# Large tiles on multiples of 256 bytes, the second pair's q and v in pools of their own, and another memory layout for the second MLP stage

## The chip, the cores and the metric

The kernel runs on one core of a Trainium2 chip. The metric is the device time of one execution in microseconds (us). Five engines matter here, with the names that the profile gives them: PE (TensorE, matrix products; PEld is its loading of the stationary operand), DVE (VectorE), ACT (ScalarE), POOL (GpSimd) and SP (SyncE, which issues most of the DMAs, in the order of its program). SBUF, the memory on the chip that the engines read and write, has 128 partitions; "address" below means a byte address within a partition.

## The reference

One encoder layer over a sequence of 1024 positions with a model width of 1024, in float32:

```
h    = RMSNorm(x)
[z | xBC | dt | q | k | v] = h @ W_in                     # 1024 x 5664
ssd  : depthwise conv of 5 taps and SiLU on xBC, Mamba-2 scan in both directions
       (8 chunks of 128, 16 heads of 64, 2 groups), + D*x, * SiLU(z), grouped RMSNorm
na   : 16 heads of 64, RMSNorm on q and k, attention of every position to an 8 x 16 window
       of the 16 x 64 grid, with a learned bias
x    = x + concat(ssd, na) @ W_out                        # 2048 x 1024
x    = x + relu(RMSNorm(x) @ W1)^2 @ W2                   # 1024 x 4096 and 4096 x 1024
```

## The kernel before

Every large product is made from float32 operands split into a high and a low part of type float32r: three matmuls (high x high, high x low, low x high) go into the same PSUM tile. In a matmul one operand is stationary (128 x 128, loaded by PEld) and one is moving (128 rows, 512 columns in the large products, which are 2048 bytes of a partition). A split costs an ACT copy (`wh`, `hTh`, the first half of `ahl`; line 367) and a subtraction on DVE or POOL (`wl`, second half of `ahl`; line 368).

Stages, in the order of time:

1. Input projection and scan (to about 620 us). The normalised input lies transposed in `hTh` and `hTl`; weights come in `wraw` tiles. The scan of the state-space part runs between the projections. `rcol` holds the norm's factor of each position and is read until the last piece of the projection is split (lines 919 and 920). `q`, `k` and `v` go to DRAM.
2. Attention for the 8 pairs of heads and three quarters of the output projection (to about 905 us). `pair_loads` fetches `q`, `k`, `kl` and `v` of a pair into one of two sets of tiles: set 0 in pool `b0`, set 1 in pool `b1`. The output projection's matmuls (`po`) take `wh`, `wl` from pool `wp` as moving and `yh`, `yl` from pool `yp` as stationary operand.
3. Last quarter of the output projection, norm, and first MLP product (to 1266 us): 8 blocks of 7 products (a Winograd form of Strassen's scheme; order 1, 2, 6, 5, 7, 3, 4) of 24 matmuls each. Moving operand `h` in the tiles `h1` to `h7` (pools `hA` and `b0`), stationary `wh`, `wl` from `wp`. The seven results of each pair of blocks are stored in `act_dr`.
4. Second MLP product (to the end): 4 blocks of 7 products of 48 matmuls. For each product two stationary pairs `ahl` come from activations (`ar`, loaded from `act_dr`), and two moving pairs `wh`, `wl` from the weights (`wraw`, for products 6, 5, 7, 4 combined by subtractions on DVE, lines 1911 to 1916). The tiles are taken from rings in turn: `ahl` from `a1`, `a1`, `a2`, `a2`, `a3`, `a3`; the weights' halves from `wy` three times and `wp` three times.

Stages 1 to the beginning of 3 are written as tasks with costs, due times and an earliest time (`since`, in us relative to the time at which PE is planned to end the stage before); a planner in the program orders them, and this order is kept on each engine. The rest of 3 and all of 4 is ordered by the framework, which simulates the engines and puts an instruction where its operands and its memory are free.

SBUF is given out from two sides. Pools of the left side stack upwards from address 4224: `cp`, `wp`, then what a stage needs (`hp`, `sp`; `x2p`; `hq`; `x1`, `a3`). Pools of the right side stack downwards from 229344: `b0` first, then `yp` and others, in stage 3 `wq` and `hA`, in stage 4 `rb`, `wy`, `x0`, `ra`, `a2`, `a1`, `ar`. A tile in a new pool waits for the users of whatever lay in its memory before. `cp` is 928 bytes long with `rcol` in it, so `wp` begins at 5152, which is 32 beyond a multiple of 256; all further large tiles of the left side that the matmuls of 512 columns read begin 32 beyond such a multiple as well. Those of the right side that the matmuls of 512 columns read begin 224 beyond one, because 229344 does, and because the sizes in between are multiples of 256.

The tiles of stage 4 lie where these of stage 3 were: `rb` on `h6` and `h5`, `wy` on the raw weights `wq`, `x0` on `h4`, `ra` on `h3`, `a2` and `a1` on `h2` and `h1`, `ar` on `h7`, `x1` and `a3` on `hq`. The first two `wraw` of stage 4 are those of `wp`.

Of the kernel before, what the change touches and what calls it, by code (L numbers as in the profile page):

```python
# [10 lines left out]
F32 = mybir.dt.float32  # L11
F32R = mybir.dt.float32r
# [7 lines left out]
P = 128  # L20
T = 1024
D = 1024
NT = T // P
# [207 lines left out]
def hymba_block(  # L231
# [27 lines left out]

    cp = ctx.enter_context(tc.tile_pool(name="cp", bufs=1))  # L260
    wp = ctx.enter_context(tc.tile_pool(name="wp", bufs=1))
    ps = ctx.enter_context(tc.tile_pool(name="ps", bufs=1, space=PSUM))
    dr = ctx.enter_context(tc.tile_pool(name="dr", bufs=1, space=DRAM))

# [130 lines left out]
        emit = lambda: nc.sync.dma_start(out(), src())  # L395
        plan.task("SP", 0.45, emit, reads=reads, writes=writes, size=size, **more)

    def tiles_of_pair(i, pool):
        make = {
            f"{t}{i}": partial(pool.tile, [P, 2, T], F32R, tag=t, name=t, bufs=1)  # L400
            for t in ("q", "k", "kl")
        }
        make[f"v{i}"] = partial(pool.tile, [P, NT, 2, P], F32R, tag="v", name="v", bufs=1)
        return make

    kls = {}
# [1 line left out]
    def pair_loads(plan, p, after=()):  # L408
        Buf, part, task = plan.buf, plan.part, plan.task
        i = p % 2  # L410
        free = dict(since=4.0) if p == 1 else {}
        q, k, v = Buf(f"q{i}"), Buf(f"k{i}"), Buf(f"v{i}")
        qp = {(j, a): part(q) for j in range(2) for a in range(2)}
        kp = [part(k) for _ in range(2)]
        for j in range(2):
            for a in range(2):
                load_task(
                plan,
                    256,
                    partial(lambda j, a: q.t[a * HD : (a + 1) * HD, j].bitcast(F32), j, a),  # L420
                    partial(lambda j, a: q_dr[p // 4, a ^ j, p % 4, j * HD : (j + 1) * HD], j, a),
                    reads=after, writes=[qp[j, a]],
                    name="q",
                    **free,
                )
            load_task(
                plan,
                512,
                partial(lambda j: k.t[j * HD : (j + 1) * HD].bitcast(F32), j),
                partial(lambda j: k_dr[p // 4, 0, p % 4].rearrange("(h d) t -> d h t", h=2), j),  # L430
                reads=after, writes=[kp[j]],
                name="k",
                **free,
            )
        if p < 2:
            kls[p] = Buf(f"kl{i}"), []
            for j in range(2):
                half_, whole = part(kls[p][0]), kls[p][0]
                kls[p][1].append(half_)
                task("POOL", 1.0, partial(lambda j, b: nc.gpsimd.memset(b.t[HD * (1 - j) : HD * (2 - j), j].bitcast(F32), 0.0), j, whole), writes=[half_], name="kl0", **free)  # L440
        kl, klp = kls[i]
        for j in range(2):
            hp = slice(HD * j, HD * j + HD)
            load_task(plan, 256, partial(lambda hp, j: kl.t[hp, j].bitcast(F32), hp, j), partial(lambda hp: k_dr[p // 4, 1, p % 4, hp], hp), reads=after, writes=[klp[j]], name="kl", **free)
        load_task(
                plan,
            1024,
            lambda: v.t.bitcast(F32).rearrange("t b h e -> t b (h e)"),
            lambda: v_dr[:, :, 2 * p : 2 * p + 2].rearrange("b t h a d -> t b (h a d)"),
            reads=after, writes=[v],  # L450
            name="v",
            **free,
        )
        return q, qp, k, kp, kl, klp, v

# [31 lines left out]
        task("ACT", 0.69, lambda: nc.scalar.activation(yh.t, pt.t, AF.Copy, scale=col), reads=[pt], writes=[yh], name="yh")  # L487
        task("DVE", 0.76, low, reads=[pt, yh], writes=[yl], due=None if due is None else due + 6, name="yl")

    def out_weights(plan, part_, h, k2, due=None):  # L490

        Buf, task = plan.buf, plan.task
        raw, w = Buf("raw"), Buf("w")
        r0 = 512 * part_ + 256 * k2

        def load():
            raw.t = wp.tile([P, 1024], F32, tag="wraw", name="wraw", bufs=2)
            nc.sync.dma_start(
                raw.t.rearrange("p (a f) -> p a f", a=2),
                w_out[0][r0 : r0 + 256, 512 * h : 512 * h + 512].rearrange("(a p) f -> p a f", p=P),  # L500
            )

        def high():
            w.t = [wp.tile([P, 1024], F32R, tag=t, name=t, bufs=3) for t in ("wh", "wl")]
            nc.scalar.activation(w.t[0], raw.t, AF.Copy)

        def low():
            nc.gpsimd.tensor_tensor(w.t[1], raw.t, w.t[0].bitcast(F32), op=sub)

        task("SP", 0.45, load, writes=[raw], size=512, name="raw")  # L510
        task("ACT", 1.06, high, reads=[raw], writes=[w], name="wh")
        task("POOL", 2.42, low, reads=[raw], writes=[w], due=due, name="wl")
        return w
# [3 lines left out]
    b0 = b0s.enter_context(tc.tile_pool(name="b0", bufs=2, side="right", reuse_waits="tile"))  # L517

    with ExitStack() as ph:
# [14 lines left out]
        dt = sp.tile([P, 2, NT, 16], F32, name="dt")  # L534


        rcol = cp.tile([P, NT], F32, name="rcol")
        p1 = ExitStack()
        rp = p1.enter_context(tc.tile_pool(name="rp", bufs=1, side="right", reuse_waits="tile"))
        rrow = rp.tile([P, T], F32, name="rrow")  # L540
# [55 lines left out]
                nc.tensor.matmul(prr, lhsT=ones, rhs=dg, start=True, stop=True)  # L596
                nc.scalar.copy(rrow[:, h * 512 : (h + 1) * 512], prr)

        prow = sp.tile([82, P], F32, name="prow", bufs=1)
        nc.sync.dma_start(prow[0:60, :], conv_w[0].rearrange("k (t p) -> (k t) p", p=P))  # L600
        nc.sync.dma_start(prow[60:72, :], conv_b[0].rearrange("(t p) -> t p", p=P))
        nc.sync.dma_start(prow[72:80, :], ssm_norm_w[0].rearrange("(t p) -> t p", p=P))
# [232 lines left out]
        for tag, n, d in LENT_TILES:  # L835
            make[tag] = partial(yp.tile, [P, 512], d, tag=tag, name=tag, bufs=n)

        make |= tiles_of_pair(0, b0)
        Buf, part, task = plan.buf, plan.part, plan.task
        stored_halves = []  # L840
        BT, CT, BH, BL = (plan.given(Buf(f"{t}0")) for t in ("q", "k", "kl", "v"))
# [331 lines left out]
        for i, key in enumerate((k, h, w) for h in range(2) for k in range(4) for w in range(2)):  # L1173
            tag, n = lent[i]
# [66 lines left out]

    with ExitStack() as ph:
        enter_phase(ph, 2, 2, 0)
        cb, yt, b1, ap = (
            pa.enter_context(
                tc.tile_pool(name=n, bufs=2, side="right", reuse_waits="tile")
            )
            for n in ("cb", "yt", "b1", "ap")
        )
        before = plan  # L1250
        plan = Plan(
# [12 lines left out]
        for pool_, tag, n, shape, d in (  # L1264
# [10 lines left out]
            (ap, "rb", 1, [P, T], F32),  # L1275
        ):
            make[tag] = partial(pool_.tile, shape, d, tag=tag, name=tag, bufs=n)
        for i, b_ in enumerate((b0, b1)):
            make |= tiles_of_pair(i, b_)

        sp = partial(load_task, plan)
        nam = Buf("nam")
# [15 lines left out]
        def w_out_part(n):  # L1298
# [8 lines left out]
                        task("ACT", 0.63, partial(lambda yh, yl: nc.scalar.activation(yh.t, yl.t.bitcast(F32), AF.Copy), yh, yl), reads=[yl], writes=[yh], name="yh")  # L1307
                        task("POOL", 1.31, partial(lambda yh, yl: nc.gpsimd.tensor_tensor(yl.t, yl.t.bitcast(F32), yh.t.bitcast(F32), op=sub), yh, yl), reads=[yh], writes=[yl], name="yl")
            for h in range(2):
                ws = first_w if n == h == 0 else [out_weights(plan, n, h, k2) for k2 in range(2)]  # L1310
                for t in range(NT):
                    pt, d = Buf("mm"), X2[t][h]
                    at = pace * (16 * n + 8 * h + t) + 6
                    for k in range(4):

                        def products(k=k, pt=pt, ws=ws, t=t):
                            yh, yl = YH[k, t // 4], YL[k, t // 4]
                            hi, lo = ws[k // 2].t
                            w, s = slice((k % 2) * 512, (k % 2) * 512 + 512), slice(t % 4 * P, (t % 4 + 1) * P)
                            mm3(pt.t, yh.t[:, s], yl.t[:, s], hi[:, w], lo[:, w], k == 0, k == 3)  # L1320

                        task("PE", 0.682, products, reads=[YH[k, t // 4], YL[k, t // 4], ws[k // 2]], writes=[pt], due=at + 0.7 * k, name="po")
                    view = x2[:, t, h * 512 : (h + 1) * 512]
                    if n == 0:
                        sp(256, partial(lambda v: v, view), partial(lambda t, h: x[0, t * P : (t + 1) * P, h * 512 : (h + 1) * 512], t, h), writes=[d], name="x", since=0.5)
                    task("DVE", 0.69, partial(lambda v, pt: nc.vector.tensor_tensor(v, v, pt.t, op=add), view, pt), reads=[pt], writes=[d], due=at + 12, name="x2")
# [212 lines left out]
    def w_split(src, eng):  # L1539
        hl = ring_tile("hl", hls, ("wh", "wl"), (F32R, F32R))  # L1540
        split_to(hl, src, eng)
        return hl

    with ExitStack() as ph:
        phase["ps"] = ph.enter_context(
            tc.tile_pool(name="ps3", bufs=1, space=PSUM, reuse_waits="tile")
# [276 lines left out]
            hc[i] = [H[i, n].t for n in range(2)]  # L1823
        nps.close()
        x2s.close()
        hq = ph.enter_context(tc.tile_pool(name="hq", bufs=1, reuse_waits="tile"))
        for fb in range(8):
            kb = (k0, k1)[fb] if fb < 2 else Block(fb)
# [14 lines left out]
    with ExitStack() as ph:  # L1843
        phase["ps"] = ph.enter_context(
            tc.tile_pool(name="ps4", bufs=1, space=PSUM, reuse_waits="tile")
        )
        rb, wy, x0, ra, a2, a1, ar_ = (
            ph.enter_context(tc.tile_pool(name=n, bufs=1, side="right", reuse_waits="tile"))
            for n in ("rb", "wy", "x0", "ra", "a2", "a1", "ar")
        )  # L1850
        x1, a3 = (
            ph.enter_context(tc.tile_pool(name=n, bufs=1, reuse_waits="tile")) for n in ("x1", "a3")
        )
        acc = [p.tile([P, NT // 2, D], F32, name="acc") for p in (x0, x1)]
        hls[:] = [wy] * 3 + [wp] * 3
        ring["hl"] = ring["raw"] = 0
        raw_a = [wp] * 2 + [ra] * 4
        raw_b = [rb] * 8
        ahl = [a1] * 2 + [a2] * 2 + [a3] * 2
        ring["rb"] = ring["ahl"] = 0  # L1860

        def raw_of(n):
            if n in ("11", "21"):
# [1 line left out]
            return ring_tile("rb", raw_b, ("wraw",), (F32,))[0]  # L1865

        def a_load(fb, i, u):
            ar = ar_.tile([P, 1024], F32, tag="ar", name="ar", bufs=4)
            nc.sync.dma_start(
                ar.rearrange("p (a t) -> p a t", a=2), act_dr[fb][i - 1, :, 2 * u : 2 * u + 2, :]  # L1870
            )
            return ar
# [8 lines left out]
        for fb in range(4):  # L1881
# [23 lines left out]
            for i in ORD:  # L1905
# [20 lines left out]
                for t in range(4):  # L1926
# [15 lines left out]
                    if fb == 3 and i in (2, 7, 3, 4):  # L1942
                        nc.sync.dma_start(
                            out[0, tt * P : (tt + 1) * P, dh * 512 : (dh + 1) * 512], d
                        )


_INS = [
# [41 lines left out]
```

## Time and profile before

| | |
|---|---|
| median of 3 runs | 1592.01 us (1591.32 to 1594.81) |
| the profiled execution | 1591.7 us, of which 1589.9 us from the first to the last instruction |
| granted TensorE clock, mean | 0.993 |
| busy | PE 1555.2 us (98%), PEld 1288.3 (81%), DVE 1009.7 (64%), POOL 730.6 (46%), ACT 722.8 (45%) |
| matmuls | 7462 |
| DMA | 278.73 MB, 175 GB/s over the span |

How to read it: busy times are unions of the instructions' spans. The end of a matmul is modelled (its span overlaps the next one's), so its pace is read from the distance of starts: a stretch's length by the number of matmuls in it. The groups give for each kind of instruction its count, its busy time, the mean of one in ns, the idle time of its engine just before it, and what ended that. In the stretches of time, each engine has its busy us with the number of its instructions (x...), then come the granted clock of PE, the mean share of time in which the 16 DMA engines were busy, and GB/s.

### The profile page before, as it was taken

Reading aid. Unit: us, or ns where it says so; the run is one execution under the profiler, and the core shown is the slowest. Engines: PE = TensorE matmul, PEld = TensorE weight load, DVE = VectorE, ACT = ScalarE, POOL = GpSimd, SP = SyncE. Lnnn points to the kernel's source line nnn. Section 1 sums busy time; section 2 is a strip of 40 time slices with the busy share of each in tenths; the row PEclk is TensorE's granted clock in tenths of the full one; section 3 lists DMA queues with packets and bytes.
Section 4 is the critical chain, followed back from the end, with each engine's and each line's share of the span. In section 5 each row is a group of like instructions: output and inputs, shape, how many; then the busy total and the mean of one; then the engine's idle time right before and its main releaser. Section 6 shows DMA issues by size and latency. Waiting matters only on the chain. (4 is left out here: it accounts for less than half of the span.)

```text
span 1589.9 us, 20811 instructions
## 1 busy us (share of the span) xinstructions
PE 1555.2 (98%) x7462; PEld 1288.3 (81%) x7462; DVE 1009.7 (64%) x1414; ACT 722.8 (45%) x1187; POOL 730.6 (46%) x530
## 2 busy tenths in 40 slices
PE   7999999999999999999999999999999989999999
PEld 5788878888878888888888777888888768888887
DVE  3776454687688855677776485444444488877763
ACT  5434323444345435667676244544444534333330
POOL 2000066765689833133363353444444474555551
PEclk9999999999999999999999999999999999999999
DMA  8212398777777795999782512444442685444232
GB/s 225 54 40 70 94 313 267 218 245 246 229 213 212 227 278 152 234 263 250 190 232 82 172 67 67 161 151 151 152 151 108 240 311 203 160 159 146 93 106 80
DMA packets 184226, 278.73 MB, mean 175 GB/s; under 512 B 14819, under 2 KB 106043, under 8 KB 184123
## 3 DMA queue, kind: packets, MB, share of 16 engines
q1 hardware_dynamic: 133323, 233.88, 49.0%
q10 hardware_dynamic: 49792, 39.85, 7.7%
q0 software_dynamic: 1008, 3.67, 0.6%
q8 instruction: 59, 0.97, 0.3%
q14 instruction: 44, 0.36, 0.1%
HBM read 191.51 MB, written 89.18 MB: 177 GB/s over the span
## 5 line engine op out<-in xcount | busy, mean ns | idle before, releaser
L368 POOL TENSOR_TENSOR wl<-wraw,wh 128x1024 fp32r<-128x1024 f32 x113 | 308.2, 2739 | 309.1 <-ACT wh L367 281.0
L367 ACT ACTIVATE wh<-wraw 128x1024 fp32r<-128x1024 f32 x125 | 131.3, 1054 | 172.7 <-PE px L1219 47.3
L362 PE MATMUL pq<-wh,hTh 128*128 128x512 f32 x512 | 204.6, 400 | 2.2 <-DVE qn L929 1.7
L363 PE MATMUL pq<-wl,hTh 128*128 128x512 f32 x512 | 200.1, 391 | 0.2 <-DVE wl L882 0.2
L364 PE MATMUL pq<-wh,hTl 128*128 128x512 f32 x512 | 200.1, 391 | 0.0
L1219 PE MATMUL px<-wh,ahl 128*128 128x512 f32 x512 | 160.6, 391 | 4.7 <-ACT ahl L367 3.4
L1219 PE MATMUL px<-h,wh 128*128 128x512 f32 x512 | 162.9, 399 | 0.6 <-ACT cq L1626 0.6
L368 DVE TENSOR_TENSOR ahl<-ar,ahl 128x1024 fp32r<-128x1024 f32 x56 | 115.3, 2065 | 22.8 <-ACT ahl L367 21.7
L367 ACT ACTIVATE ahl<-ar 128x1024 fp32r<-128x1024 f32 x56 | 58.3, 1052 | 140.4 <-PE px L1219 74.7
L1219 PEld LDWEIGHTS px<-wh,ahl 128*128 128x128 f32 x512 | 96.0, 188 | 26.2 <-ACT ahl L367 3.9
L1219 PEld LDWEIGHTS px<-h,wh 128*128 128x128 f32 x512 | 96.2, 189 | 24.1 <-ACT cq L1626 0.8
L362 PEld LDWEIGHTS pq<-wh,hTh 128*128 128x128 f32 x512 | 96.2, 188 | 22.2 <-DVE qn L929 2.1
L364 PEld LDWEIGHTS pq<-wh,hTl 128*128 128x128 f32 x512 | 96.1, 188 | 20.6
L363 PEld LDWEIGHTS pq<-wl,hTh 128*128 128x128 f32 x512 | 96.3, 188 | 19.5 <-DVE wl L882 0.7
L1219 PE MATMUL px<-h,wl 128*128 128x512 f32 x256 | 101.4, 396 | 0.0
L1219 PE MATMUL px<-wl,ahl 128*128 128x512 f32 x256 | 99.7, 390 | 0.0
L1404 DVE CUSTOM_DVE_ANT_0 pr<-psc,mb 128x384 f32<-128x384 f32 (+1 forms) x128 | 64.8, 520 | 28.7 <-PE psc L1401 21.1
L1416 ACT ACTIVATE pr<-pr,nmx 128x384 f32<-128x384 f32 (+1 forms) x128 | 74.5, 583 | 18.7 <-DVE nmx L1404 18.1
L362 PE MATMUL po<-wh,yh 128*128 128x512 f32 x192 | 80.9, 421 | 0.0
L1219 PE MATMUL pz<-wh,ahl 128*128 128x512 f32 x256 | 80.5, 390 | 0.0
L1219 PE MATMUL pz<-h,wh 128*128 128x512 f32 x256 | 80.4, 394 | 0.0
L1438 DVE TENSOR_TENSOR ptl<-ptp,pth 128x384 fp32r<-128x384 f32 (+1 forms) x128 | 65.5, 521 | 23.2 <-ACT pth L1440 22.3
(332 smaller groups left out, 3748.7 us busy)
## 6 DMA issues: line engine op xcount, KB each, us to landing
ar<-act_dr SPq DMA_DIRECT2D x56, 512.0 KB, 3.9
act_dr<-cq SPq DMA_DIRECT2D x49, 512.0 KB, 2.7
wraw<-in_w_in_dram SPq DMA_DIRECT2D x44, 512.0 KB, 6.5
rb<-cum_dr SPq DMA_DIRECT2D x32, 512.0 KB, 6.3
wraw<-in_w_mlp_in_dram SPq DMA_DIRECT2D x32, 512.0 KB, 3.9
wraw<-in_w_mlp_out_dram SPq DMA_DIRECT2D x32, 512.0 KB, 4.9
q_dr<-hl ACTq DMA_DIRECT2D x16, 512.0 KB, 4.8
k_dr<-hl ACTq DMA_DIRECT2D x16, 512.0 KB, 3.6
```

The lines of the kernel that those rows point to most:

```text
L362: nc.tensor.matmul(pt, lhsT=ah, rhs=bh, start=first, stop=False)
L363: nc.tensor.matmul(pt, lhsT=ah, rhs=bl, start=False, stop=False)
L364: return nc.tensor.matmul(pt, lhsT=al, rhs=bh, start=False, stop=last)
L367: nc.scalar.activation(hl[0], src, AF.Copy)
L368: eng.tensor_tensor(hl[1], src, hl[0].bitcast(F32), op=sub)
L1219: nc.tensor.matmul(pt, lhsT=a, rhs=b, start=f, stop=l, skip_group_check=True)
L1404: nc.vector.tensor_tensor_reduce(pr.t[:, 0:n], pt.t[:, 0:n], mb.t[:, o : o + n], scale=-1.0, scalar=3.0e38, op0=add, op1=ALU.min, accum_ou ...
L1416: nc.scalar.activation(pr.t[:, 0:n], pr.t[:, 0:n], AF.Exp, bias=nmx.t[:, b : b + 1], scale=-1.0, accum_out=den.t[:, hh, b : b + 1],)
L1438: nc.vector.tensor_tensor(lo[0], pv3, hi.bitcast(F32), op=sub)
```

## The change

No instruction is added or removed; tiles are moved, and the order of some instructions changes with them.

- `rcol` goes from `cp` to `sp`, so that `wp` begins at 5120. An unused tile of 224 bytes, `top`, is put first on the right side, so that `b0` ends at 229120. Both are multiples of 256, and so are the starts of the large tiles stacked on them. `prow` goes from `sp` to `rp`. The tiles `xt` of the first 25 us, which lie below `rp`, begin 192 beyond a multiple of 256 after it and 160 before it.
- `q` and `v` of set 1 get pools of their own, `bq` and `bv`, at the addresses that they had within `b1`. The earliest times of their first loads (pair 1) go from 4.0 to -10 (`q`) and -8 (`v`); those of `k` and `kl` stay at 4.0. The two loads of output weights for the second half of the first quarter get the earliest times 1.0 and 2.0, where they had none.
- Stage 4 gets the pools `ra`, `wa`, `rb`, `x0`, `wb`, `a2`, `a1`, `arb` on the right, and `arp`, 16 KB, on the left, opened where `x2` has been, before `hq`. Adding up their sizes: `ra` now lies on `h5`, `wa` on `h6`, `rb` (6 tiles) on `wq`, `x0` on `h4` as before, `wb` on `h3`, `a2` and `a1` on `h2` and `h1` as before, `arb` on half of `h7`. The first two `wraw` and the first two `ar` of stage 4 are in `arp`. The ring of the weights' halves is `wa` twice, `wb` twice, `wp` three times; the last two of the eight tiles of `rb`'s ring are in `wp`.

```diff
     wp = ctx.enter_context(tc.tile_pool(name="wp", bufs=1))
+    top = ctx.enter_context(tc.tile_pool(name="top", bufs=1, side="right"))
+    top.tile([P, 56], F32, name="top")
...
-    def tiles_of_pair(i, pool):
+    def tiles_of_pair(i, pool, q_pool, v_pool):
         make = {
-            f"{t}{i}": partial(pool.tile, [P, 2, T], F32R, tag=t, name=t, bufs=1)
+            f"{t}{i}": partial(q_pool.tile if t == "q" else pool.tile, [P, 2, T], F32R, tag=t, name=t, bufs=1)
             for t in ("q", "k", "kl")
         }
-        make[f"v{i}"] = partial(pool.tile, [P, NT, 2, P], F32R, tag="v", name="v", bufs=1)
+        make[f"v{i}"] = partial(v_pool.tile, [P, NT, 2, P], F32R, tag="v", name="v", bufs=1)
...
                     name="q",
-                    **free,
+                    since=-10.0 if p == 1 else -1e3,
...
             name="v",
-            **free,
+            since=-8.0 if p == 1 else -1e3,
...
-    def out_weights(plan, part_, h, k2, due=None):
+    def out_weights(plan, part_, h, k2, due=None, since=-1e3):
...
-        task("SP", 0.45, load, writes=[raw], size=512, name="raw")
+        task("SP", 0.45, load, writes=[raw], size=512, name="raw", since=since)
...
-        rcol = cp.tile([P, NT], F32, name="rcol")
+        rcol = sp.tile([P, NT], F32, name="rcol")
...
-        prow = sp.tile([82, P], F32, name="prow", bufs=1)
+        prow = rp.tile([82, P], F32, name="prow", bufs=1)
...
-        cb, yt, b1, ap = (
+        cb, yt, bv, bq, b1, ap = (
...
-        for i, b_ in enumerate((b0, b1)):
-            make |= tiles_of_pair(i, b_)
+        make |= tiles_of_pair(0, b0, b0, b0) | tiles_of_pair(1, b1, bq, bv)
...
-                ws = first_w if n == h == 0 else [out_weights(plan, n, h, k2) for k2 in range(2)]
+                ws = first_w if n == h == 0 else [out_weights(plan, n, h, k2, since=1.0 + k2 if n == 0 else -1e3) for k2 in range(2)]
...
         x2s.close()
+        arp = arps.enter_context(tc.tile_pool(name="arp", bufs=1, reuse_waits="tile"))
         hq = ph.enter_context(tc.tile_pool(name="hq", bufs=1, reuse_waits="tile"))
...
-        rb, wy, x0, ra, a2, a1, ar_ = (
+        ra, wa_, rb, x0, wb_, a2, a1, arb = (
             ph.enter_context(tc.tile_pool(name=n, bufs=1, side="right", reuse_waits="tile"))
-            for n in ("rb", "wy", "x0", "ra", "a2", "a1", "ar")
+            for n in ("ra", "wa", "rb", "x0", "wb", "a2", "a1", "arb")
         )
...
-        hls[:] = [wy] * 3 + [wp] * 3
-        ring["hl"] = ring["raw"] = 0
-        raw_a = [wp] * 2 + [ra] * 4
-        raw_b = [rb] * 8
+        hls[:] = [wa_] * 2 + [wb_] * 2 + [wp] * 3
+        raw_a = [arp] * 2 + [ra] * 4
+        raw_b = [rb] * 6 + [wp] * 2
+        raw_x = [arp] * 2 + [arb] * 2
         ahl = [a1] * 2 + [a2] * 2 + [a3] * 2
-        ring["rb"] = ring["ahl"] = 0
+        for n in ("hl", "raw", "rb", "ar", "ahl"):
+            ring[n] = 0
...
-            ar = ar_.tile([P, 1024], F32, tag="ar", name="ar", bufs=4)
+            ar = ring_tile("ar", raw_x, ("ar",), (F32,))[0]
```

More of the change, by code (lines that the diff above doesn't have):

```diff
@@ L836, in hymba_block @@
             make[tag] = partial(yp.tile, [P, 512], d, tag=tag, name=tag, bufs=n)
-        make |= tiles_of_pair(0, b0)
+        make |= tiles_of_pair(0, b0, b0, b0)
         Buf, part, task = plan.buf, plan.part, plan.task
@@ L1247, in hymba_block @@
             )
-            for n in ("cb", "yt", "b1", "ap")
+            for n in ("cb", "yt", "bv", "bq", "b1", "ap")
         )
@@ L1542, in w_split @@
         return hl
+    arps = ExitStack()
     with ExitStack() as ph:
@@ L1945, in hymba_block @@
                         )
+    arps.close()
 _INS = [
```

## The prediction

> **What bounds the kernel now.** I read the page first, then the stretches of time, then PE's waits, then the distance of PE's matmuls in each stage.
>
> ```profile
> PE 1555.2 (98%) x7462; PEld 1288.3 (81%) x7462; DVE 1009.7 (64%) x1414; ACT 722.8 (45%) x1187; POOL 730.6 (46%) x530
> ```
>
> PE is the bound nearly everywhere: 34.7 of 1589.9 us are idle. So a change gains only by ending PE's waits or by letting its matmuls follow each other faster. For the second I compare the starts of matmuls of one shape (512 columns, float32r, every one with a new stationary operand). Stage 3, from the order of time on PE; the rows between are 24 matmuls of `py` and 24 of `px`:
>
> ```profile
> 1232.66 0.63 PE L1219 MATMUL py<-h,wh 128*128 128x512 f32 x2
> ...
> 1243.86 0.63 PE L1219 MATMUL pz<-h,wh 128*128 128x512 f32 x2
> ```
>
> 48 matmuls in 11.20 us: 233.3 ns each. Stage 4, from the chain of waits that ended last (start, length, what):
>
> ```profile
> 1301.35 10.89 PE px L1219 x48
> 1312.24 10.89 PE pz L1219 x48
> 1323.13 11.06 PE px L1219 x48
> 1334.19 10.92 PE pz L1219 x48
> ...
> 1388.87 11.07 PE pz L1219 x48
> ```
>
> The same 48 matmuls take 10.89 us, 226.9 ns each, and at every third product 11.06 or 11.07. Now count the rings. A product takes two places of each ring of six, so product n (from 0) takes places 2n and 2n+1. For n = 0, 3, ... both operands lie on the right (both 224 beyond a multiple of 256), for n = 2, 5, ... both on the left (both 32 beyond); for n = 1, 4, 7, ... one of its two weight tiles is in `wp` (32) and both `ahl` in `a2` (224). 1323.13 is n = 4 and 1388.87 is n = 10. So the slow products are those in which half of the matmuls have a moving and a stationary operand of unlike offset: 0.18 us for 24 matmuls, 7.5 ns each. In stage 3 all have it (`h` at 224, `wh` and `wl` at 32) and all are 6.4 ns slower. I read this as a cost of the two operands' offset of 64 bytes, modulo 256, to each other.
>
> Where stage 4 begins, PE waits and its clock falls (stretches of time: us, PE, PEld, DVE, ACT, POOL busy, granted clock, DMA share, GB/s):
>
> ```profile
> 1266.27:1312.24 45.97, 36.74 (x146) 28.98 (x146) 37.85 (x25) 19.26 (x20) 31.01 (x14) 0.93 0.88 318
> 1312.24:1586.04 273.80, 273.79 (x1200) 224.83 (x1199) 198.14 (x172) 91.38 (x93) 133.55 (x45) 1.00 0.40 136
> ```
>
> Stage 3's last matmul ends its turn at 1266.27; stage 4's first three products, 144 matmuls, take until 1312.24. At 226.9 ns they would take 32.7 us, so 13.3 are lost, 0.2 of them to offset and 13.1 to waits and the clock after them. The other 25 products lose nothing else.
>
> **The change part by part.** No instruction comes or goes.
>
> *Offsets.* `wp` goes from 5152 to 5120, and the right side ends at 229120: every large tile is then at offset 0, so moving and stationary agree as they do in the 226.9 ns products. No other engine is near to taking PE's place in stages 3 and 4: beside a full PE, DVE has 198 of 274 us in the last row above, and in stage 3 the gap of 10.21 us that is shown below. In stage 3 there are 8 x 7 x 24 = 1344 such matmuls; the first 72 (products 1 and 2 of the first block, 1 of the second) stand among the norm's transposes, where PE waits for DVE, and count nothing. 1272 x 6.4 ns = 8.2 us. Stage 4 has nine slow products of 28: 9 x 0.18 = 1.6 us. In stage 2, `po` has its moving operand in `wp` (32) and its stationary in `yp` (224). A run of it without other work, from the order of time on PE:
>
> ```profile
> 869.56 0.39 PE L362 MATMUL po<-wh,yh 128*128 128x512 f32 x1
> ...
> 881.92 0.39 PE L362 MATMUL po<-wh,yh 128*128 128x512 f32 x1
> ```
>
> 54 matmuls in 12.36 us, 228.9 ns: 2.0 ns over 226.9. For 576 of them 1.2 us (ends: 0, and 3.7 at stage 3's 6.4 ns). Sum of the offsets: 11.0 us. The projections of stage 1 have both operands on the left at 32 and keep their pace.
>
> *The beginning of stage 4.* What PE waited for, and what DVE and SP did then (order of time; idle time before it and what ended that in brackets):
>
> ```profile
> 1269.87 0.50 PE L1219 MATMUL px<-wh,ahl 128*128 128x512 f32 x1 [3.45 <-ACT ahl L367]
> ...
> 1273.27 0.73 PE L1219 MATMUL px<-wh,ahl 128*128 128x512 f32 x2 [1.30 <-DVE ahl L368]
> ...
> 1289.92 1.22 PE L1219 MATMUL py<-wh,ahl 128*128 128x512 f32 x2 [4.27 <-DVE ahl L368]
> ```
>
> ```profile
> 1249.42 2.57 DVE L1911 TENSOR_TENSOR wraw<-wraw 128x1024 f32<-128x1024 f32 x1 [10.21 <-PE pz L1219]
> ...
> 1272.00 4.56 DVE L368 TENSOR_TENSOR ahl<-ar,ahl 128x1024 fp32r<-128x1024 f32 x2
> 1276.49 3.41 DVE L1916 TENSOR_TENSOR wraw<-wraw 128x1024 f32<-128x1024 f32 x1
> 1279.83 3.42 DVE L368 TENSOR_TENSOR ahl<-ar,ahl 128x1024 fp32r<-128x1024 f32 x1
> 1283.17 3.42 DVE L1916 TENSOR_TENSOR wraw<-wraw 128x1024 f32<-128x1024 f32 x1
> 1286.51 3.35 DVE L368 TENSOR_TENSOR ahl<-ar,ahl 128x1024 fp32r<-128x1024 f32 x1
> ```
>
> ```profile
> 1255.25 0.81 SPq L1869 DMA_DIRECT2D ar<-act_dr  x2
> 1260.85 1.08 SPq L1894 DMA_DIRECT2D wraw<-in_w_mlp_out_dram  x2
> ```
>
> The first `ar` is loaded at 1255.25, when product 7 of stage 3's last block gives `h7` back (products begin 5.60 us apart from 1227.07; the third begins at 1238.27, the fifth at 1249.46). Its split stands behind the block's last sums on ACT and DVE, and DVE then has no gap until 1289.9. After the change the first two `ar` and `wraw` lie in `arp`, free since the norm; `a1` is free at 1238, `wa` (on `h6`) at 1244. All of product 1's splits can lie in DVE's idle 10.21 us and on POOL, which is 46% busy on the page. Product 2's weights load into `ra` from 1249 instead of 1260.85, and their halves go to `wb` when `h3` is free at 1260.7. The four `ahl` subtractions, 4.56 + 3.42 + 3.35 = 11.3 us, leave DVE's full stretch, and so do the waits of 3.45 and 1.30. Late next is stage 4's third product, due at 1266.3 + 21.8 = 1288.1: its `ahl` go to `a3`, on `cq` tiles whose stores are issued last at 1272. Those stores are POOL's (median to landing 9.8 us on the page), so ACT starts at about 1282, and two splits with DVE at 1.2 to 3.4 us each end between 1286 and 1291. I leave 4 us for this wait and the clock behind it, and take 9 of 13.1. Ends: 0, if the framework keeps the splits behind the sums, and 13.1.
>
> *The second pair.* PE's waits on a DMA (total us, times, longest), the stretches of time around the second one, and what SP and ACT did before it:
>
> ```profile
> PE ptn L575 <- DMA xt<-in_x_dram: 5.8, 7, 2.2
> ...
> PE pv L1368 <- DMA q<-q_dr: 2.3, 1, 2.3
> ```
>
> ```profile
> 630.00:640.00 10.00, 10.00 (x60) 8.91 (x59) 7.79 (x21) 6.49 (x18) 2.29 (x3) 1.00 1.06 231
> 640.00:650.00 10.00, 7.73 (x40) 6.58 (x39) 4.91 (x15) 4.33 (x12) 2.39 (x3) 0.85 1.08 244
> 650.00:660.00 10.00, 10.00 (x58) 8.91 (x57) 6.79 (x19) 6.02 (x17) 0.00 (x0) 0.97 1.04 206
> 660.00:670.00 10.00, 10.00 (x62) 8.94 (x61) 6.79 (x20) 6.86 (x19) 4.81 (x4) 1.00 1.07 259
> ```
>
> ```profile
> 615.88 2.74 SPq L498 DMA_DIRECT2D wraw<-in_w_out_dram  x2
> ...
> 635.70 1.98 SPq L395 DMA_DIRECT2D q<-q_dr  x2
> ```
>
> ```profile
> 617.32 0.69 ACT L919 ACTIVATE rb<-pq,rcol 128x512 fp32r<-128x512 f32 x1 [1.55 <-PE pq L364]
> ```
>
> Against 61 matmuls in 10 us, 24 are missing in two rows: 3.9 us with the lower clock. SP stood before the `wraw` loads of 615.88 until POOL's `wl` gave their buffers back, with pair 1 behind them. After, `q` is planned ahead of them and waits at the head of SP only for the last users of its memory (`qn` and `hl`, the stores of the last piece of `k`); `v` waits there for `rcol`, which the last piece's split reads at 617.32 on ACT and then on DVE. Behind `v` stand `x`, `k`, `kl` and the weights, as `x` and pair 1 stood behind the weights until 618.6. 1 MB of `q` is then out of a stretch whose DMA share is over 1, about 4 us at 244 GB/s, against a wait of 2.3. I take 3 of the 3.9 (nearer to that row than to a new wait); ends: 3.9, and -2 if `kl` or `x` is late instead by as much. That transfers as such get cheaper I cost at nothing: the other wait is on `xt`, at no multiple of 256 after either.
>
> *Sum.* 11.0 + 9 + 3 = 23.0 us from the profiled 1591.7, which is 0.3 below the median of 1592.0: 1569 us.
>
> **The rivals.**
>
> (a) *The pace has nothing to do with the multiple of 256.* In every slow case one operand is on the left and the other on the right, so the distance in memory could be what costs. For this: no row shows unlike offsets on one side. Against: 64 bytes are 16 elements, and 16 columns at 226.9 / 512 = 0.44 ns are 7.1 ns, what a matmul loses (6.4 and 7.5). Then the 11 us do not come, and the new rings, seven against six, put operands on different sides in 10 of 21 matmuls of stage 4 (640 instead of 216), 424 x 7.5 ns = 3.2 us more: 1591.7 - 9 - 3 + 3 = 1583; 1580 without this. [...]
>
> (b) *The start of stage 4 does not gain.* The framework orders by its simulation and may leave product 1's splits where they are, or DVE is full up to the third product. Then 11.0 + 3 come: 1578. Against: DVE's idle 10.21 us, and the weights' splits, which it did put ahead of the sums.
>
> (c) *Slower: the sides now differ by 256 modulo 512.* 229120 is 447.5 times 512, 5120 is ten times 512. Before, tiles of one side always were multiples of 512 apart; the two sides were 64 off. If the cost grows with the distance within 512 bytes, 6.4 ns for 64 make 26 for 256: 19.2 ns more on 1272 matmuls (24.4 us), 23.6 on 576 (13.6), and 14.8 in stage 4 (640 x 25.6, less the 1.6): 1591.7 + 53 - 12 = 1633. It decides where 2488 matmuls cost what is gained elsewhere and offsets cost now (12 + 11): from 9.2 ns at 256 bytes. Nothing in the trace excludes it.
>
> (d) *Nothing moves*: the pace stays and the waits return elsewhere, 1592.
>
> **How the numbers follow.** Forecast 0.58 (1561 to 1575), (a) 0.17, (b) 0.14, (c) 0.06, (d) 0.05. The low end is all gains at their upper ends, 8.2 + 1.6 + 3.7 + 13.1 + 3.9 = 30.5: 1561; the high end takes in (b) and (a): 1583. Faster by over 0.2% (3.2 us, about what a measurement of this kernel tells from no change) is the forecast, (a) and (b): 0.89. Same 0.05, slower 0.06.
>
> **What would show it.** Offsets: stage 3's 48 matmuls in 10.89 us instead of 11.20, and stage 4's products all at 10.89, also where the rings mix sides; 11.20 speaks for (a), over 11.6 for (c). Start of stage 4: `ar` loads long before 1255, `ahl` subtractions in DVE's idle time before the block's last sums, no PE wait for the first `ahl`; a wait of some us at the third product. Second pair: `q` loads before 600, no wait at 646. Wrong makes it a pace that does not follow the offset, or a new wait in stage 2, whose order is planned anew.

## The result and the profile after

The changed kernel takes 1581.81 us (median of 7 executions, 1580.55 to 1589.21), the kernel before beside it 1594.81 us (7 executions). The ratio on record is 0.994, 95% interval [0.9925, 0.9955], about 9.6 us less; the two medians lie 13.0 us apart. I forecast 23. Measured once more (`again` below) the ratio was 0.9944 [0.9923, 0.9964], with medians 7.8 us apart, so the gain is clear of the noise, and I take it as about 9 us. The execution profiled for the changed kernel is its longest (1589.21 us, span 1587.4); a second one (`again`) has 1580.27 and a span of 1578.5. One of the six executions of `offs` below is slow (3998.12 us) and is left out of its median and its ratio.

The page's row of busy time, as before nearly all PE:

```profile
PE 1548.1 (98%) x7462; PEld 1291.3 (81%) x7462; DVE 1013.5 (64%) x1414; ACT 720.9 (45%) x1187; POOL 730.3 (46%) x530
```

Stage 3 after, from the order of time on PE: the same 48 matmuls take 10.88 us instead of 11.20.

```profile
1232.05 0.62 PE L1221 MATMUL py<-h,wh 128*128 128x512 f32 x2
...
1242.93 0.62 PE L1221 MATMUL pz<-h,wh 128*128 128x512 f32 x2
```

Stage 4 after, from the chain of waits that ended last: from the sixth product on 10.88 each (x96 is two of them). No product of 11.06 is left, though the rings now mix the sides in 576 of 1344 matmuls (216 before; the prediction's 640 took a share of 10 in 21 that holds over 21 products, and there are 28).

```profile
1333.33 10.88 PE pz L1221 x48
1344.21 21.76 PE px L1221 x96
1365.97 10.88 PE py L1221 x48
...
1572.69 10.89 PE px L1221 x48
```

What PE waited for (total us, times, longest):

```profile
PE po L365 <- POOL wl L510: 3.9, 2, 3.2
PE pv L1369 <- ACT pth L1441: 3.3, 1, 3.3
...
PE px L1221 <- ACT ahl L369: 3.1, 1, 3.1
...
PE px L1221 <- DVE cq L1633: 2.7, 1, 2.7
```

The wait on `q` at 646 is gone. The first two rows are new and lie in stage 2, at 670 to 678 us; below, their stretch is called the stop. The last two are the beginning of stage 4, where one wait has been traded for another. Set against the kernel before, matmul by matmul, the start of PE's matmuls moves like this: -2.6 us where the second pair begins, +9.2 between 668 and 690 us, -8.0 over stage 3, +0.5 from stage 3 to stage 4, -1.5 over the rest of stage 4.

### The profile page after: what moved, and what is told of

Its sections match the earlier page's. It is cut to its first block, busy times and chain, and to the rows that moved or that the text cites. A ratio compares the mean times of both kernels' runs of the same rounds, so it can differ in the third digit from the quotient of the medians.

```text
span 1587.4 us, 20805 instructions
## 1 busy us (share of the span) xinstructions
PE 1548.1 (98%) x7462; PEld 1291.3 (81%) x7462; DVE 1013.5 (64%) x1414; ACT 720.9 (45%) x1187; POOL 730.3 (46%) x530
## 2 busy tenths in 40 slices
DMA packets 184226, 278.73 MB, mean 176 GB/s; under 512 B 14819, under 2 KB 106043, under 8 KB 184123
## 3 DMA queue, kind: packets, MB, share of 16 engines
q0 software_dynamic: 1008, 3.67, 0.6%
```

## Experiments

**The offsets by themselves.** `offs` is the kernel before with

```
+    top = ctx.enter_context(tc.tile_pool(name="top", bufs=1, side="right"))
+    top.tile([P, 56], F32, name="top")
-        rcol = cp.tile([P, NT], F32, name="rcol")
+        rcol = sp.tile([P, NT], F32, name="rcol")
-        prow = sp.tile([82, P], F32, name="prow", bufs=1)
+        prow = rp.tile([82, P], F32, name="prow", bufs=1)
```

> The kernel before with the offsets alone moved (top of 224 bytes on the right, rcol out of cp, prow beside it); all engines execute the same instructions in the same order as before. Theory A (pace follows the two operands' offset to each other modulo 256 bytes): stage 3's 48 matmuls in 10.89 us instead of 11.20, stage 4's products all 10.89, 10 us less: 1582 to 1585. Rival (the pace belongs to the new rings or to the new order): 11.20 and 1592 to 1595, as before.

`nooffs` is the changed kernel with the same lines taken back.

> The changed kernel without the offsets alone (large tiles again at 32 on the left and 224 on the right, modulo 256); same instructions in the same order as after. Theory A: stage 3's 48 matmuls in 11.20 us, stage 4's products that mix the sides 10.9 to 11.25, together 8.2 + 4.5 us more than after: 1593 to 1600, slower than before or equal to it. Rival (the pace comes with the order): stays at 10.89 and within 2 us of after.

`rel128` and `rel32` are `offs` with `[P, 24]` and `[P, 48]` instead of `[P, 56]`.

> As the offsets alone, but the right side's large tiles begin 128 bytes beyond a multiple of 256, the left side's at a multiple (before: 192 bytes apart, or 64 the other way). Same order as before. If the cost grows with the distance to the next multiple of 256 (64 bytes: 6.4 ns), 13 ns a matmul: stage 3's 48 in 11.5 us and the whole 8 us over before, about 1602. If every distance that isn't a multiple costs the same: 11.20 and 1592 to 1595. If only 64 bytes matter (a multiple of 128 is good enough): 10.89 and 1582 to 1585.

> As the offsets alone, but with the right side's large tiles 32 bytes beyond a multiple of 256 and the left side's at a multiple; same order as before. One look at the pace in stage 3. With 64 bytes (before) it was 233.3 ns a matmul, with 128 bytes 232.4, with 0 226.7. If what counts is whether the offset is 0 or not: 232 to 234. If it grows up to 64 bytes and stays: about 230. If steps of 32 are harmless: 226.7.

Medians, beside 1591.69 us of the kernel before: `offs` 1577.83 (5 executions, 1576.58 to 1580.26), ratio 0.9912 [0.9892, 0.9932]; `nooffs` 1594.40, 1.0019 [1.0001, 1.0037]; `rel128` 1588.41, 0.9986 [0.997, 1.0003]. `rel32` ran once, for its profile: 1591.65. Stage 3 in each, first and last row of 48 matmuls on PE; `offs`:

```profile
1224.06 0.62 PE L1221 MATMUL py<-h,wh 128*128 128x512 f32 x2
...
1234.93 0.62 PE L1221 MATMUL pz<-h,wh 128*128 128x512 f32 x2
```

`nooffs`:

```profile
1195.21 0.63 PE L1219 MATMUL py<-h,wh 128*128 128x512 f32 x2
...
1206.41 0.63 PE L1219 MATMUL pz<-h,wh 128*128 128x512 f32 x2
```

`rel128`, and below it `rel32`:

```profile
1189.86 0.62 PE L1221 MATMUL py<-h,wh 128*128 128x512 f32 x2
...
1201.00 0.64 PE L1221 MATMUL pz<-h,wh 128*128 128x512 f32 x2
```

```profile
1193.83 0.63 PE L1221 MATMUL py<-h,wh 128*128 128x512 f32 x2
...
1205.03 0.63 PE L1221 MATMUL pz<-h,wh 128*128 128x512 f32 x2
```

10.87, 11.20, 11.14 and 11.20 us. Since `offs` and the kernel before run the same instructions in the same order, and `nooffs` and the changed kernel too, the pace belongs to the offsets and to nothing else in the change. The cost does not grow with the distance: 226.7 ns a matmul at distance 0, 233.3 at 32 and at 64 bytes, 232.4 at 128 (stage 3). Nor is the distance all that counts. In stage 4 of `nooffs`, by the order of its rings, the product at 1368.75 has all its moving operands at 224 and all its stationary ones at 32, as stage 3 has, and the next one has them the other way round, as `po` has:

```profile
1368.75 11.20 PE py L1219 x48
1379.95 11.00 PE px L1219 x48
```

233.3 ns and 229.2 at the same 64 bytes; `po` had 228.9. So the other way round 64 bytes cost 2.5 ns and not 6.6. The second reading is as plain: the offsets alone gain more than the whole change. What else was changed costs 3 us without the offsets (1.0019) and some 5 with them (0.9944 against 0.9912).

**Once more, as it is.** `again` is the changed kernel without an edit.

> The changed kernel once more, unchanged, for a profile of one more execution. Theory A (the 9.2 us of new waits at 668 to 690 us are in every execution, since the weights' raw loads are now held back there): median 1582 to 1589, PE again busy for only 13 to 14 us of 660 to 680, waits on `wl` and `pth` of about 3 us each. Theory B (those waits belong to that one execution, which was the slowest of seven): the wait is under 2 us and the profiled time is near 1581.

1583.91 us median, 1580.27 to 1585.97. The profiled execution took 1580.27 and has no stop at 668 to 690; neither A nor B, since the other executions lie between it and the 1589.21 that had the stop. Where it comes from is seen on the queues. The changed kernel as first profiled, SP, POOL, ACT and PE in order of time:

```profile
660.10 0.34 SPq L397 DMA_DIRECT2D braw<-t_dr  x1
...
666.28 0.38 SPq L500 DMA_DIRECT2D wraw<-in_w_out_dram  x1
```

```profile
667.93 2.38 POOL L1336 TENSOR_TENSOR mb<-braw,nam 128x384 f32<-128x384 f32 x3 [9.68 <-DVE nmx L1405]
670.28 2.33 POOL L510 TENSOR_TENSOR wl<-wraw,wh 128x1024 fp32r<-128x1024 f32 x1
```

```profile
676.26 1.06 ACT L507 ACTIVATE wh<-wraw 128x1024 fp32r<-128x1024 f32 x1 [10.26 <-DMA wraw<-in_w_out_dram]
```

```profile
672.67 0.50 PE L365 MATMUL po<-wl,yh 128*128 128x512 f32 x1 [3.17 <-POOL wl L510]
677.74 0.48 PE L1369 MATMUL pv<-pth,v 128*128 128x256 f32 x1 [3.29 <-ACT pth L1441]
```

The same instructions in `again`, SP and POOL:

```profile
655.47 0.34 SPq L397 DMA_DIRECT2D braw<-t_dr  x1
...
660.84 0.38 SPq L500 DMA_DIRECT2D wraw<-in_w_out_dram  x1
```

```profile
662.57 2.41 POOL L1336 TENSOR_TENSOR mb<-braw,nam 128x384 f32<-128x384 f32 x3 [8.79 <-DVE x L1327]
664.94 2.39 POOL L510 TENSOR_TENSOR wl<-wraw,wh 128x1024 fp32r<-128x1024 f32 x1
```

SP is 5 us behind in the first: `braw` lands at 667.8 instead of 662.4, POOL has `mb` ahead of `wl` and waits, so `wl` is 5 us late and PE stops for `po`; then ACT stands for 10.26 us at `wh`, whose raw load was issued 5 us late too, with `pth` queued behind it, and PE stops again. The program is the same; what differs is how far the transfers have come: from 620 to 655 us 9.01 MB are moved in the first and 9.52 in `again`.

**The parts.** `pairs` is `offs` with the second pair's lines (own pools and `since` for `q` and `v`, `since` for the weights) and the old layout of stage 4; `lay` is `offs` with the new layout and the old second pair.

> The kernel before with the offsets and the second pair's part (q and v in own pools and ahead, the weights' raw loads held back), with the old layout of stage 4. With the offsets alone the ratio to before was 0.9912, with the whole change 0.9944. Theory P (the second pair's part gives back what the offsets bring: no wait on q at 646 any more, but `wl` or `pth` 3 us late at 670 to 690 in most executions): 1581 to 1585, as the whole change. Theory L (the layout of stage 4 gives it back): 1576 to 1579, at or under the offsets alone by the 2 to 3 us of the wait on q.

> The kernel before with the offsets and the new layout of stage 4, without the second pair's part. Theory P: the layout moves the waits where stage 4 begins but not their sum, 1577 to 1580, as the offsets alone. Theory L: 1581 to 1585. My prediction's term for the beginning of stage 4 (9 us less) would give 1568 to 1571.

`pairs` 1582.04, 0.9936 [0.9913, 0.9959]; `lay` 1581.07, 0.9925 [0.9904, 0.9945]; the kernel before 1592.27. Neither gains over the offsets alone; the intervals overlap, so how the 5 us divide stays open between them. The profile of `pairs` has the stop (5.8 us later between 668 and 702), `lay` has none.

**What the stop hangs on.** `nosince` takes back the holding of the weights, `p2late` holds the third pair back instead, `rate255` changes the planner's rate:

```
nosince: -out_weights(plan, n, h, k2, since=1.0 + k2 if n == 0 else -1e3)
         +out_weights(plan, n, h, k2)
p2late:  free = ... dict(since=44.0) if p == 2; q, v: since=... 44.0 if p == 2
rate255: -moved = max(moved, at + 1.5) + t.size / 290.0
         +moved = max(moved, at + 1.5) + t.size / 255.0
```

> The changed kernel without holding the weights' raw loads back (q and v stay ahead of them). Theory W (those two loads come too late: issued at 667 to 673 in a stretch where the DMA share is over 1, and ACT stands in order at their split): the stop at 670 to 690 is gone in every execution, 1577 to 1580, and the executions lie closer together. Rival (the early q and v themselves crowd that stretch): 1582 to 1586, with another wait there.

> The changed kernel with the third pair's loads (p = 2: q, k, kl, v) planned from about 656 us on instead of from 643. Theory S (SP's queue: they stand ahead of `braw` and of the weights' raw in a stretch where the DMA share is over 1, and POOL's `mb` and ACT's `wh` wait in order for those): `braw` and the raw loads are issued 5 us earlier, the stop at 668 to 690 is gone, 1577 to 1580, the executions within 5 us of each other. Rival (the third pair is then late itself): a wait of PE on q, k or v at 685 to 700 of 3 us or more, 1583 to 1588.

> The changed kernel with the planner's rate for transfers at 255 instead of 290 GB/s (640 to 680 us shows 212 to 333, mean 262). Theory R (the plan puts `po`, `mb` and `wh` of 665 to 680 where they are because it counts on 290 GB/s): no wait of PE over 1 us between 640 and 700, 1576 to 1580. Rival (any new order of a crowded stretch has some other latecomer): a wait of 2 us or more elsewhere in stage 2 and 1582 to 1588.

`nosince` 1584.82, 0.9954 [0.9938, 0.9969]: theory W falls. The raw loads go out at 617 and 619 and PE still waits 3.1 us for `wl`, since POOL's `mb` stands ahead of it and its `braw` goes out at 660.00. `p2late` 1580.51, 0.9923 [0.99, 0.9945], executions from 1578.57 to 1582.54: the stop is gone and the executions lie close together, as theory S has it, with the median half a us above its range. One profile without the stop would not show this, since `again` has none either; the narrow spread does, and `pairs_p2` below, with the same hold, has it too (1578.58 to 1581.29, against 1577.62 to 1586.51 of `pairs`). Its POOL and SP:

```profile
661.76 2.41 POOL L1336 TENSOR_TENSOR mb<-braw,nam 128x384 f32<-128x384 f32 x3 [8.47 <-DVE nmx L1405]
665.07 2.41 POOL L510 TENSOR_TENSOR wl<-wraw,wh 128x1024 fp32r<-128x1024 f32 x1 [0.90 <-ACT wh L507]
```

```profile
650.96 0.38 SPq L500 DMA_DIRECT2D wraw<-in_w_out_dram  x1
...
653.32 0.33 SPq L397 DMA_DIRECT2D braw<-t_dr  x1
```

With the third pair's loads behind them, the raw load goes out 15 us and `braw` 7 us earlier than in the first profile. `rate255` took 1628.13 us (1.0225): the plan of stage 1 changed with it and PE was 47 us later by 592 us, with 11.5 us of waits for `qn`. It says nothing on stage 2.

**The beginning of stage 4.** `pin` and `nosplit` are the changed kernel with

```
pin:     last = nc.vector.tensor_tensor(s4, c21, s2, op=sub)      # stage 3's last sum
         with tc.issue_after(last.ins):                           # if fb == 0
             nc.vector.tensor_tensor(q["12"], q["22"], q["12"], op=sub)
nosplit: ah = ar.bitcast(F32R)                                    # if fb == 0 and i == 1
         wa.append(((ah, ah), w_split(src, nc.gpsimd)))
```

> The changed kernel with DVE's two weight differences for stage 4's fifth product (wraw, issued before the last block's sums) kept behind the last sum of stage 3. Theory D (they delay the sums by 4.6 us, and with them PE and ACT's `ahl`): no wait of PE for `cq` (2.7 before), `ahl` on ACT 3 us earlier, 3 to 5 us less than the changed kernel: 1579 to 1581. Rival (ACT's order puts `ahl` behind the last product's copies whatever DVE does): the wait for `cq` goes and the wait for `ahl` grows by as much, 1582 to 1585.

> The changed kernel in which stage 4's first product reads the loaded `ar` in place of both halves of `ahl` (its two splits, 2 copies on ACT and 2 subtractions on DVE, are left out). It shows what early splits of product 1 could bring at most. Theory F (the late splits of product 1 are what holds the beginning of stage 4): PE's waits for `ahl` there (3.2 + 1.5 us) go with the low clock after them, 5 to 8 us less than the changed kernel: 1575 to 1579. Rival (DVE is full up to the third product): the wait comes back at product 2 or 3 and 2 us or less are gained: 1580 to 1584.

`pin` 1581.94, 0.9931 [0.9908, 0.9955]; `nosplit` 1584.22, 0.9946 [0.9925, 0.9967]: both as the changed kernel, at or near the rivals' ranges. `nosplit` leaves two splits out and gains nothing. PE's waits in `pin`, then in `nosplit`:

```profile
PE py L1221 <- DVE ahl L370: 4.3, 2, 4.1
PE px L1221 <- ACT ahl L369: 3.5, 1, 3.5
```

```profile
PE py L1221 <- DVE ahl L370: 6.5, 2, 3.5
```

The wait for `cq` goes in `pin` and one of 4.1 us for product 2's `ahl` comes; where product 1 needs no split at all, product 2 waits 6.5 us for DVE. DVE in `nosplit` (stretches of time, columns as in the prediction):

```profile
1270.00:1280.00 10.00, 6.50 (x29) 5.10 (x28) 10.00 (x5) 5.23 (x6) 9.94 (x8) 1.00 0.83 320
1280.00:1290.00 10.00, 7.00 (x21) 5.28 (x21) 9.87 (x8) 0.00 (x0) 4.12 (x2) 0.73 0.77 249
```

DVE is full from 1270 to 1290. Not by the amount of its work alone: POOL is busy for 9.94 of the first 10 us, and in the kernel before the five 128x1024 subtractions of DVE that lie wholly beside POOL's `wl`, from 1273 to 1290, take 3.35 to 3.43 us, where one alone takes 1.21 (1263.31). That this stretch of DVE sets the sum is argued from these rows; no run kept POOL's `wl` out of it.

**What the second pair's part brings without the stop.** `offs2` is `offs` again, `pairs_p2` is `pairs` with the lines of `p2late`.

> The offsets alone once more, for a second profile and more executions. Theory Q (the wait on `q` at 646 that the second pair's part takes away is already small or absent in most executions once the offsets are moved, since the same transfers take less time): a profile at 1576 to 1579 with less than 1 us of idle PE between 640 and 660. Rival (it is there in each): 2 to 4 us of idle PE between 640 and 650, as in the first profile of this kernel.

> The offsets and the second pair's part, with the third pair's loads planned from about 656 us on and with the old layout of stage 4. If the stop at 668 to 690 is all that the second pair's part costs and the wait on `q` is there in most executions without it: 1575 to 1577, 2 us under the offsets alone. If that wait is mostly absent (theory Q): 1577 to 1580, as the offsets alone.

`offs2` 1576.45, 0.9907 [0.9888, 0.9925]; `pairs_p2` 1580.12, 0.9925 [0.991, 0.9941]; the kernel before 1591.75. This profile is as theory Q has it. `offs2` at 640, where the kernel before idles 2.27 us:

```profile
640.00:650.00 10.00, 10.00 (x61) 8.90 (x61) 6.91 (x21) 6.56 (x19) 2.42 (x3) 1.00 1.04 251
```

and what the DMA engines did from 620 to 690, in the kernel before and then in `offs2` (packets and rate; the queue of SP and ACT with packets, MB and share of 16 engines):

```profile
DMA packets 8244, 16.82 MB, mean 240 GB/s; under 512 B 795, under 2 KB 3499, under 8 KB 8239
...
q1 hardware_dynamic: 8095, 16.23, 102.1%
```

```profile
DMA packets 10292, 20.33 MB, mean 290 GB/s; under 512 B 954, under 2 KB 4826, under 8 KB 10285
...
q1 hardware_dynamic: 10141, 19.72, 101.5%
```

Both are full, and the second moves 21% more. But that the offsets take the wait on `q` away is not shown. The same matmul at 646 in `offs`, `rel128` and `rel32`:

```profile
646.29 0.33 PE L1370 MATMUL pv<-ptl,v 128*128 128x128 f32 x1 [1.80 <-DVE ptl L1440]
```

```profile
645.83 0.33 PE L1370 MATMUL pv<-ptl,v 128*128 128x128 f32 x1 [0.32 <-DVE ptl L1440]
```

```profile
646.08 0.33 PE L1370 MATMUL pv<-ptl,v 128*128 128x128 f32 x1 [0.49 <-DMA q<-q_dr]
```

The first profile of `offs` still idles 1.8 us (18.38 MB from 620 to 690), while `rel128` and `rel32`, whose right side is off the multiples, idle 0.3 and 0.5 and move 17.41 and 17.07 MB, little more than the 16.82 of before. One order, five profiles, and the wait goes from 0 to 2.3 us without following the offsets; only one execution of the kernel before has a profile, so how often it waits there is open. What is shown is that the second pair's part isn't needed for the wait to be small. And where it is in, PE comes 2.6 us ahead of the kernel before between 630 and 668 in nine profiles, against 0.5 (`offs`), 2.7 (`lay`), 3.1 (`rel32`), 3.5 (`rel128`) and 4.1 (`offs2`) without it. Of all that was run, the offsets alone are the best kernel: some 14 us under the kernel before, 5 under the changed one.

## Why the prediction was right and wrong

*Offsets: right in stages 3 and 4 in what they gain.* Stage 3 gave 8.0 us (8.2 forecast), stage 4 1.5 (1.6). Rivals (a) and (c) are refuted: sides are mixed and 256 bytes apart modulo 512, and from stage 4's sixth product on every product takes 10.88 us; in stage 3 a matmul went from 233.3 to 226.7 ns. `po` was mis-sized: 1.2 forecast, 0.6 between 702 and 914 us (kernel before to `offs2`).

Two arguments about the cause don't stand. The prediction put the slow products' 0.18 us on the 24 matmuls of unlike offset, 7.5 ns each. In the slow product that it shows at 1388.87 the first six matmuls, all alike, start 226.7 ns apart, and the other 42, in turns of six unlike and six alike, 231.4 on the mean, the alike ones as slow as the unlike: a matmul's own two operands don't settle its pace, and that the sum came out is luck. And it read 64 bytes as the time of 16 columns, 7.1 ns; 32 bytes cost as much.

*Offsets: the step "That transfers as such get cheaper I cost at nothing" was wrong about the transfers, and its price stays open.* From 590 to 910 us a MB costs the 16 engines 3.57 and 3.48 us of packet time in `offs` and `offs2`, 3.68 to 3.79 in the kernel before, `rel128` and `rel32`. The offsets gave 13 to 15 us instead of 11, and in `offs2` 4.1 of them come between 630 and 668, at the wait on `q`; but in `rel128` and `rel32`, with dearer transfers, 3.5 and 3.1 come there too. So where the 2 to 4 us over the forecast come from isn't shown. Nor do the times of single packets follow the multiples everywhere: in stage 3 a 4096-byte packet has a median of 159 ns before and after, and from 620 to 690 its mean is 307 in the kernel before and 257 in `offs2`, but 290 in `nooffs` without the multiples and 295 in the changed kernel with them.

*Second pair: the step "I take 3 of the 3.9" failed.* The wait is gone and 2.6 us come, but most of it can go without this part too. And the end "-2 if `kl` or `x` is late instead by as much" looked at the data of pair 1 only, not at the small `braw` and the weights behind it on SP: POOL's `mb` and ACT's `wh` wait for them in order, with `wl` and `pth` behind, and PE loses 9.2 us between 668 and 690 in one profile of the changed kernel and 0.6 in the other. I did name a new wait in stage 2 as what would make the prediction wrong, and gave it no term.

*The beginning of stage 4, the largest miss (9 us forecast, none came): the step "All of product 1's splits can lie in DVE's idle 10.21 us" failed; rival (b) came, both halves of it.* The loads came early, as forecast (in `again` the two `ar` of product 1 at 975 and 1008 us). The framework did not put the splits there. DVE and POOL after, in order of time:

```profile
1253.54 2.82 DVE L1916 TENSOR_TENSOR wraw<-wraw 128x1024 f32<-128x1024 f32 x1
1256.28 3.42 DVE L1918 TENSOR_TENSOR wraw<-wraw 128x1024 f32<-128x1024 f32 x1
1259.62 3.42 DVE L1916 TENSOR_TENSOR wraw<-wraw 128x1024 f32<-128x1024 f32 x1
1262.96 1.21 DVE L1918 TENSOR_TENSOR wraw<-wraw 128x1024 f32<-128x1024 f32 x1
1264.09 0.67 DVE L1633 TENSOR_TENSOR cq<-cq,px 128x512 f32<-128x512 f32 x1
...
1275.89 4.53 DVE L370 TENSOR_TENSOR ahl<-ar,ahl 128x1024 fp32r<-128x1024 f32 x2
```

```profile
1249.53 12.42 POOL L370 TENSOR_TENSOR wl<-wraw,wh 128x1024 fp32r<-128x1024 f32 x4 [3.03 <-ACT wh L369]
```

The idle time was filled with differences of weights, which the early raw loads made ready. They run beside POOL's four `wl` and take 2.8 to 3.4 us where the last, alone, takes 1.21. So the sums of stage 3 come late (PE waits 2.7 us for `cq`) and `ahl` at 1275.89, later than the 1272.00 of before. PE's loss from the last two products of stage 3 to stage 4's sixth product, over 226.7 ns a matmul (before 233.3 in stage 3), summed from the starts of its matmuls:

| kernel | ahead of product 1 | products 1 to 3 | 4 and 5 | 6 | sum |
|---|---|---|---|---|---|
| before | 3.6 | 9.6 | 0.2 | 0.0 | 13.4 |
| `offs` | 3.9 | 9.0 | 0.0 | 0.2 | 13.1 |
| after | 7.9 | 5.2 | 1.0 | 0.0 | 14.1 |
| `lay` | 7.9 | 3.2 | 6.0 | 0.0 | 17.1 |
| `pin` | 3.7 | 9.1 | 0.0 | 0.0 | 12.8 |
| `nosplit` | 3.0 | 10.0 | 0.0 | 0.0 | 13.0 |

The loss moves, and its sum stays at 12.8 to 14.1, or grows (`lay`). Loads that come early don't lower it, and neither does leaving out product 1's splits (`nosplit`). What is left as the bound is DVE, busy for 19.87 of 20 us from 1270 to 1290 in `nosplit`, with subtractions that, in the kernel before, take 3.4 us beside POOL's `wl` and 1.21 alone; that is argued, not tested. My 9 us took one wait away without asking what DVE had to do up to the third product.

*Sum.* Forecast 11 + 9 + 3. Measured: offsets 13 to 15, beginning of stage 4 and second pair together some 5 lost. That the whole came out at 1581.8, near rival (b)'s 1578, is luck: errors that partly cancel.

## What to carry to other kernels

Let moving and stationary operands of float32r matmuls have the same start modulo 256 bytes: here it cost one tile of 224 bytes and gave 3% of the pace in stage 3, where they differed by 64 bytes (233.3 to 226.7 ns a matmul). Where one wait is removed by bringing loads forward in a stretch with a DMA share of 1, look for what is queued behind them on the issuing queue, the small loads first, and price that (here 9.2 us in one profile). Before you count on an engine's idle time, add up all that becomes ready for it by then (here 10.21 us of DVE were counted on, and differences of weights filled them).

## What was not expected of the hardware

- The pace of 512-column float32r matmuls, each with its own stationary operand, depends on where the two operands start relative to each other modulo 256 bytes: 226.7 ns where they agree, 232 to 233 at 32 and 128 bytes of distance, at 64 bytes 233 with the moving operand at 224 and the stationary at 32, and 229 the other way round. Why, no run here shows.
- With every large tile at a multiple of 256 bytes the same 278.73 MB take less of the DMA engines: all packets together 897 to 910 us of 16 engines in the twelve profiles with the offsets moved (897 to 902 in nine, 908 to 910 in `pin`, `nosplit` and `rate255`), 912 to 916 in the four others (before, `nooffs`, `rel128`, `rel32`). Most of the saving lies between 590 and 910 us (in the first profile of the changed kernel 10.9 of 15.7: 61.75 MB there, at 3.62 us a MB instead of 3.79). Its cause is open, and so is what it is worth to PE.
- One program, unchanged, cost PE 9.2 us at 668 to 690 in one execution and 0.6 in another (`again`).
